# A hybrid decoder layer on one core: two-operand elementwise work moved to VectorE, and the loads of the merge moved

## The chip, the core and the metric

The kernel runs on one core of a Trainium2 chip. The metric is the device time of one execution in microseconds. A core has a matrix engine (TensorE, PE in the profile, its weight loads PEld), a vector engine (VectorE, DVE), a scalar engine (ScalarE, ACT), a general engine (GpSimd, POOL) and a sync engine (SyncE, SP), which here only issues DMA transfers. Each engine works off its own list of instructions in order and waits on semaphores for the others.

## The reference

One decoder layer is computed for a prompt of 2048 tokens and for 8 samples of 8 new tokens, 2112 tokens in all, with model width 1024. Cut to what matters:

```
h = rmsnorm(x, norm_attn);  p = h @ w_in          # 4608 columns: q, k, v, rwkv inputs, gates
o_attn = window attention with sinks(q, k, v)      # window 128, 8 heads, 2 kv heads
o_rwkv = rwkv7_mixer(p[rwkv part], state)          # recurrence, group norm, output gate
gates = sigmoid(p[gate part] + b_gate)
merged = gates[:1024] * (o_attn @ w_branch_attn) + gates[1024:] * (o_rwkv @ w_branch_rwkv)
x = x + merged @ w_out
u = rmsnorm(x, norm_ffn) @ w_ffn_in                # 2 x 2816 columns: gate half, value half
c = cb + causal conv of width 3 over the gate half
x = x + (gelu(c) * value half) @ w_ffn_out
y = rmsnorm(x, norm_final)                         # and the new caches and states
```

## The kernel before, in words

**Blocks and halves.** Everything is kept transposed, features on the 128 partitions and tokens along the free axis. The 2112 tokens are three blocks of 704, each in two halves of 384 and 320 tokens (HALF). A matmul of the large products is one 128x128 piece of weights against 384 or 320 columns.

**Split operands.** Float32 accuracy is had from a faster float format by splitting each operand into a rounded part (hi) and the rest (lo): `mm3` (L366) runs hi·hi, hi·lo and lo·hi for each of 8 pieces of weights, 24 matmuls for a bank (`psd`, three of them). `unit` brings 128x1024 weights: SP loads them to `wr` (L346), ScalarE makes hi with a cast (L347), and lo = raw − hi is a TENSOR_TENSOR (an instruction with two full operands) at L353. Every third unit's lo is one 128x1024 instruction on VectorE, the other two units' lo are two 128x512 instructions each on GpSimd. Activations are split by `split`, a cast at L357 and a subtraction at L358. There are two buffers for `wr` and two for the split weights `wp`, so a unit is split while the unit ahead of it is multiplied: 48 matmuls, 24 for each half.

**Stages.** `start` and `inputs(0..2)` compute the projections of the three blocks (matmuls named psd<-h). Then for each block come `branches` (the products with w_branch, psd<-o, and the gated sum: two `m` tiles from L1364, their addition at L1367, hi at L1369, lo at L1370), `merge` (the product with w_out, L1400, and the second norm) and `ffn_stage` (w_ffn_in, the conv and gelu, w_ffn_out at L1470), and last the final norm, whose scaling of the last block uses VectorE at L1538 and GpSimd at L1531.

**Background work.** Attention, the triangular inverses of the rwkv mixer (L1088, L1090, and two 128x1024 transposes on VectorE at L1094 and L1096 at the end of each of six), the recurrence over chunks and the group norm are Python generators in queues called streams. A recording layer (`tick`, `step`, `account`) weaves their instructions in between the matmuls of the stages when the program is written; it estimates each engine's time with the numbers in `cost` and takes a next step where these estimates leave room. `drain` runs a stream to its end, with nothing between its steps when no stage is being written. The order on every engine is thus fixed when the program is built.

**Around the merge of block 0.** The outputs of attention (`od`) and of the rwkv mixer (`rd`) go through DRAM. `gather` loads them as eight `ol` tiles (L1316, four buffers) and splits each into `os_` (L357, L358). For block 0 the stream "c" holds, during the third projections, `chunks(0)` and the first two query tiles of `attention(1)`; `gathered(0)` is pushed on it behind them, the last four gate products are written, and `drain("c")` ends it all. The rest of attention and the work of blocks 1 and 2 follow in the merge and the FFN. For blocks 1 and 2 the generator `ahead` gathers within the FFN of the block before. `load_x1` loads the residual x of the block with four DMAs when the third weight unit of `branches` is issued (L1376). The x after an FFN is stored to `xd` by a DMA that ScalarE issues (L1486), one for each half, and the final norm reads it back later.

## Time and profile before

| | |
|---|---|
| median of 3 runs | 3327.91 us (3327.47 to 3331.76) |
| profiled execution | 3327.79 us, its span 3326.0 us |
| mean granted clock of TensorE | 0.988 of full speed |
| PE busy | 3250.5 us (98%), 24072 matmuls |
| DVE busy | 1948.6 us (59%), 4058 instructions |
| ACT busy | 1213.4 us (36%) |
| POOL busy | 1010.1 us (30%) |

Read busy shares with the clock beside them: a matmul at the lower clock level counts as busy for twice as long. A row of a timeline holds neighbouring instructions of one line: start, elapsed time, engine, line, operation, tiles and shapes, count, and in brackets the idle time before it and who ended it. "ACTq" and "SPq" rows are the engines' issuing of DMAs; "DMA x<-y" as a releaser is the landing of a transfer.

### The profile page before, as it was taken

To read this page: it belongs to the slowest core of one execution; us is meant where nothing else is said; L and a number is where in the kernel's file an instruction comes from. 1 tells how busy PE (TensorE), PEld (TensorE's weight loads), DVE (VectorE), ACT (ScalarE), POOL (GpSimd) and SP (SyncE) were. 2 spreads that over 40 slices of the span, in tenths; PEclk is the share of its full clock that TensorE was granted. 3 is DMA by queue.
4 is the path that set the end of the run, shared out by engine and by line. 5 is a ranking of instruction groups with operands and counts; after the bars stand their busy time and mean duration, and the time that the engine had idled before them with its cause. 6 is when DMAs were issued, how large, how long until landed. Compare 5 with 4: busy or idle time off the path is not lost.

```text
span 3326.0 us, 60594 instructions
## 1 busy us (share of the span) xinstructions
PE 3250.5 (98%) x24072; PEld 3131.5 (94%) x24072; DVE 1948.6 (59%) x4058; ACT 1213.4 (36%) x2274; POOL 1010.1 (30%) x878
## 2 busy tenths in 40 slices
PE   8999998999999899999999999999999999999998
PEld 8998998999999789899999999999999999999998
DVE  7676568735563466577455558745456465444545
ACT  4455433333333567523232333332233233222223
POOL 3332433323223244132222254222122353222223
PEclk9999999999999899999999999999999999999999
DMA  4643443545653744233532363253313272122222
GB/s 136 182 141 117 140 152 118 146 130 159 200 171 119 221 144 118 73 80 105 153 118 87 111 225 96 82 168 110 112 65 130 70 257 70 64 70 70 70 65 75
DMA packets 335164, 408.96 MB, mean 123 GB/s; under 512 B 110496, under 2 KB 261152, under 8 KB 334624
## 3 DMA queue, kind: packets, MB, share of 16 engines
q1 hardware_dynamic: 330720, 399.31, 38.8%
q10 hardware_dynamic: 4160, 5.77, 0.5%
q8 instruction: 190, 3.11, 0.4%
q14 instruction: 94, 0.77, 0.1%
HBM read 307.55 MB, written 98.41 MB: 122 GB/s over the span
## 4 chain that ended last, share of the span: by engine, by line
PE 71%; DVE 3%; DMA 1%; issue 1%; ACT 0%; POOL 0%; SPq 0%; POOLq 0%; DVEq 0%; ACTq 0%
PE psd L366 62%; PE psr L694 1%; PE psr L743 1%; PE psc L1162 1%; PE psc L1195 1%; PE psc L1192 1%; DVE qt L1088 1%; DVE qb L1090 1%; PE psr L730 1%; DMA xd<-x 0%; PE psr L992 0%; PE psc L1019 0%; PE psc L1197 0%; PE psc L1291 0%; PE psc L1189 0%
## 5 line engine op out<-in xcount | busy, mean ns | idle before, releaser
L366 PE MATMUL psd<-o,wp 128*128 128x320 f32 (+1 forms) x8640 | 1453.6, 326 | 21.1 <-ACT o L357 10.8
L366 PEld LDWEIGHTS psd<-o,wp 128*128 128x128 f32 x8640 | 1400.9, 189 | 32.6 <-ACT o L357 11.8
L353 POOL TENSOR_TENSOR wp<-wr,wp 128x512 fp32r<-128x512 f32 x470 | 648.1, 1400 | 1675.7 <-ACT wp L347 1595.9
L366 PE MATMUL psd<-h,wp 128*128 128x320 f32 (+1 forms) x5184 | 918.1, 330 | 15.2 <-ACT wp L347 7.4
L366 PEld LDWEIGHTS psd<-h,wp 128*128 128x128 f32 x5184 | 838.4, 190 | 30.8 <-ACT wp L347 7.4
L347 ACT CAST wp<-wr 128x1024 fp32r<-128x1024 f32 x354 | 370.6, 1047 | 647.7 <-PE psd L366 587.6
L366 PE MATMUL psd<-ff,wp 128*128 128x384 f32 (+1 forms) x3168 | 526.7, 325 | 0.0
L366 PEld LDWEIGHTS psd<-ff,wp 128*128 128x128 f32 x3168 | 510.8, 188 | 3.1 <-DVE up L1434 0.2
L1470 DVE TENSOR_TENSOR x<-x,psd 128x384 f32<-128x384 f32 (+1 forms) x288 | 148.2, 519 | 236.9 <-PE psd L366 236.7
L1441 DVE TENSOR_TENSOR gb<-psd,rb 128x64 f32<-128x64 f32 (+2 forms) x154 | 70.5, 470 | 241.2 <-PE psd L366 223.7
L353 DVE TENSOR_TENSOR wp<-wr,wp 128x1024 fp32r<-128x1024 f32 x119 | 148.1, 1244 | 88.5 <-ACT wp L347 84.7
L1444 DVE SCALAR_TENSOR_TENSOR cc<-gb,pt,cc 128x704 f32<-128x704 f32 (+1 forms) x132 | 165.1, 1251 | 33.8 <-ACT cc L1442 33.0
L1442 ACT ACTIVATE cc<-gb,pt 128x64 f32<-128x64 f32 (+2 forms) x154 | 95.7, 636 | 188.6 <-DVE gb L1441 187.2
L407 POOL TENSOR_TENSOR acc<-acc,sq 128x320 f32<-128x320 f32 (+1 forms) x93 | 95.0, 1023 | 115.5 <-ACT sq L406 97.4
L1453 ACT ACTIVATE cc<-cc 128x704 f32<-128x704 f32 x66 | 52.4, 793 | 189.0 <-DVE cc L1444 119.1
L358 DVE TENSOR_TENSOR ff<-cc,ff 128x384 fp32r<-128x384 f32 (+1 forms) x132 | 92.9, 706 | 47.0 <-ACT ff L357 46.6
L1434 DVE TENSOR_TENSOR up<-psd,rb 128x384 f32<-128x384 f32 (+1 forms) x132 | 68.6, 520 | 51.7 <-PE psd L366 51.3
L357 ACT CAST ff<-cc 128x384 fp32r<-128x384 f32 (+1 forms) x132 | 63.9, 486 | 78.7 <-DVE cc L1456 78.1
L1090 DVE TENSOR_TENSOR qb<-qb,qt 128x31 f32<-128x31 f32 (+15 forms) x186 | 88.9, 478 | 4.1
L1088 DVE TENSOR_TENSOR qt<-nb,qb 128x31 f32<-128x31 f32 (+15 forms) x186 | 84.6, 455 | 3.2
L1367 POOL TENSOR_TENSOR m<-m 128x384 f32<-128x384 f32 (+1 forms) x48 | 48.8, 1018 | 118.4 <-DVE m L1364 85.2
L1456 DVE TENSOR_TENSOR cc<-cc,up 128x384 f32<-128x384 f32 (+1 forms) x132 | 71.2, 542 | 16.7 <-ACT cc L1453 13.5
(257 smaller groups left out, 3124.2 us busy)
## 6 DMA issues: line engine op xcount, KB each, us to landing
wr<-in_w_fi SPq DMA_DIRECT2D x132, 512.0 KB, 3.5
wr<-in_w_in SPq DMA_DIRECT2D x108, 512.0 KB, 4.0
wr<-in_w_fo SPq DMA_DIRECT2D x66, 512.0 KB, 3.5
cm<-md SPq DMA_DIRECT2D x33, 512.0 KB, 4.8
gt<-gd SPq DMA_DIRECT2D x48, 352.0 KB, 4.4
md<-m SPq DMA_DIRECT2D x48, 256.0 KB, 3.4
wr<-in_w_br SPq DMA_DIRECT2D x24, 512.0 KB, 4.7
wr<-in_w_out SPq DMA_DIRECT2D x24, 512.0 KB, 3.6
```

Of the source, the lines that this page charges most:

```text
L347: nc.scalar.copy(w[:, 0], raw)
L353: eng.tensor_tensor(w[:, 1, sl], raw[:, sl], w[:, 0, sl].bitcast(F32), op=ALU.subtract)
L358: (eng or self.nc.vector).tensor_tensor(lo, src, hi.bitcast(F32), op=ALU.subtract)
L366: nc.tensor.matmul(ps[:, :n], w[:, a, wk * 128:(wk + 1) * 128], act[:, k0 + k, b, c0:c0 + n], start=(start and k == 0 and j == 0), stop=(s ...
L407: eng.tensor_tensor(acc, acc, sq[:, :n], op=ALU.add)
L1088: nc.vector.tensor_tensor(tv, nb[:, s + 1:, s:s + 1].to_broadcast([P, k, s + 1]), qb[:, s:s + 1, :s + 1].to_broadcast([P, k, s + 1]), op=A ...
L1090: nc.vector.tensor_tensor(qb[:, s + 1:, :s + 1], qb[:, s + 1:, :s + 1], tv, op=ALU.add)
L1441: nc.vector.tensor_tensor(dst, view(ps, 0), view(rb, c0), op=ALU.mult)
L1442: nc.scalar.activation(view(c, c0), dst, ACT.Identity, bias=self.par("cb", f), scale=cw[2])
L1444: nc.vector.scalar_tensor_tensor(c[:, :npr], gb[:, u:u + npr], cw[u], c[:, :npr], op0=ALU.mult, op1=ALU.add)
L1456: nc.vector.tensor_tensor(cv, cv, up[:, c0:c0 + n], op=ALU.mult)
L1470: nc.vector.tensor_tensor(xv, xv, ps[:, :n], op=ALU.add)
```

## The change

1. All two-operand elementwise work that GpSimd did goes to VectorE: the lo of every weight unit (now one 128x1024 instruction), the splits of `parts`, `q2` and `h`, the additions of squares into `acc` for the norms, the products `kp` and `kb` of the mixer, and the addition of the two `m` tiles. Only the final norm's scaling of the last block stays on GpSimd. The estimates in `cost` and `account` drop their entries for such work on GpSimd.
2. For block 0 the eight `ol` loads are a generator of their own (`load_out`, now eight buffers), queued behind `chunks(0)` in the third projections in the place of the first part of attention(1); the splits (`gather`) are drained ahead of the last four gate products. Attention(1) runs whole in the merge.
3. `load_x1` loads one quarter of x at each of the units j = 2 to 5 of `branches` instead of all four at j = 2.
4. `gate_tiles` is a plain function that asks for its first two tiles when it is called, in the FFN, and no longer at the first `next`.
5. The copy of the window caches (`wks`, `wvs`) moves from the end of the third projections to the last FFN stage, and the `kt` tile of `mtile` comes from one pool for all blocks.

```diff
@@ unit, split, square
-        eng = nc.gpsimd if self.nw % 3 else nc.vector
-        self.nw += 1
-        step = 1024 if eng is nc.vector else 512
-        for u in range(0, 1024, step):
-            sl = slice(u, u + step)
-            eng.tensor_tensor(w[:, 1, sl], raw[:, sl], w[:, 0, sl].bitcast(F32), op=ALU.subtract)
+        nc.vector.tensor_tensor(w[:, 1], raw, w[:, 0].bitcast(F32), op=ALU.subtract)
...
-        (eng or self.nc.vector).tensor_tensor(lo, src, hi.bitcast(F32), op=ALU.subtract)
+        self.nc.vector.tensor_tensor(lo, src, hi.bitcast(F32), op=ALU.subtract)
...
-        eng.tensor_tensor(acc, acc, sq[:, :n], op=ALU.add)
+        self.nc.vector.tensor_tensor(acc, acc, sq[:, :n], op=ALU.add)
@@ account
-                start = max(t[engine], t["PE"])
-                if engine == "Pool" and type(ins).__name__ == "InstTensorTensor":
-                    self.locked = start, start + c
...
-                t[engine] = start + c
+                t[engine] = max(t[engine], t["PE"]) + c
@@ gather
+    def load_out(self, b, pool, bufs):
+
+        for k in range(8 + bufs - 1):
+            if k < 8:
+                t = pool.tile([P, T], F32, tag="ol", name="ol", bufs=bufs)
+                self.nc.sync.dma_start(t, self.od[b][:, k] if k < 4 else self.rd[b][k - 4])
+                self.ols.append(t)
+            if k >= bufs - 2:
+                yield
+
+    def gather(self, os_, loads):
+
         for k in range(8):
...
+            next(loads, None)
             yield 0.0 if k else 4.0
+            t = self.ols.popleft()
@@ branches
-            if j == 2:
-                self.load_x1(b, x)
+            if 2 <= j < 6:
+                self.load_x1(b, x, 2 * j - 4)
...
-                nc.gpsimd.tensor_tensor(m[0][:, :n], m[0][:, :n], m[1][:, :n], op=ALU.add)
+                nc.vector.tensor_tensor(m[0][:, :n], m[0][:, :n], m[1][:, :n], op=ALU.add)
@@ run
-            self.inputs(2, ep, [self.chunks(0), self.attention(1, 0, 256)], HOLD)
+            lp = []
+
+            def preload():
+                lp.append(self.pool("ol", side="right"))
+                yield from self.load_out(0, lp[0].__enter__(), 8)
+
+            self.inputs(2, ep, [self.chunks(0), preload()], HOLD)
...
-        self.push("c", self.gathered(0, os_))
+        self.drain("c")
+        self.push("c", self.gather(os_, iter(())))
...
-            self.push("c", self.attention(1, 256), self.attention(2), self.inverses(1), self.chunks(1))
+            self.push("c", self.attention(1), self.attention(2), self.inverses(1), self.chunks(1))
```

**TensorE where block 0's merge begins.** Before: the end of the gate products (psd<-h), the rest of the background (L992 of the mixer, L730 and L743 of attention), and the first products of `branches` (psd<-o).

```order
L366 MATMUL psd<-h,wp 128x320 x5
L992 MATMUL psr<-ar,kb 128x128
L730 MATMUL psr<-ct,s 128x128 x8
L743 MATMUL psr<-pT,v 64x256 x2
L730 MATMUL psr<-ct,s 128x128 x4
L743 MATMUL psr<-pT,v 64x256 x2
L730 MATMUL psr<-ct,s 128x128 x4
L743 MATMUL psr<-pT,v 64x256 x4
L366 MATMUL psd<-o,wp 128x384 x13
L366 MATMUL psd<-o,wp 128x320 x13
```

Now (L354 is `mm3`, L681 the scores of attention, L978 the mixer):

```order
L978 MATMUL psr<-ar,kb 128x128
L354 MATMUL psd<-h,wp 128x384 x13
L354 MATMUL psd<-h,wp 128x320 x24
...
L354 MATMUL psd<-h,wp 128x384 x24
L354 MATMUL psd<-h,wp 128x320 x24
L354 MATMUL psd<-o,wp 128x384 x24
L354 MATMUL psd<-o,wp 128x320 x24
L354 MATMUL psd<-o,wp 128x384 x24
L354 MATMUL psd<-o,wp 128x320 x8
L681 MATMUL psr<-k_12760,q_12759 128x256 x12
```

Before, 25 background matmuls stand alone between the last gate product and the first branch product; now gate and branch products stand next to each other, and attention(1) begins among the branch products.

**SyncE's queue at the same place.** Before (ol are the outputs to be gathered, k, v and q the tiles of attention, x the residual):

```order
L1316 DMA ol<-od_226 128x704 x4
L671 DMA v<-vd_224 128x128
L665 DMA q<-qd_218 64x4x128 x3
L1316 DMA ol<-rd_0_282 128x704
L1316 DMA ol<-rd_1_283 128x704
L665 DMA q<-qd_218 64x4x128
L1316 DMA ol<-rd_2_284 128x704
L671 DMA v<-vd_224 128x128
L1316 DMA ol<-rd_3_285 128x704
L671 DMA v<-vd_224 128x128
L1376 DMA x_12723<-in_xT 128x2x704 x4
L346 DMA wr<-in_w_br 128x1024
```

Now:

```order
L1281 DMA rd_3_284<-y 128x320
L1303 DMA ol<-od_225 128x704 x4
L1303 DMA ol<-rd_0_281 128x704
L1303 DMA ol<-rd_1_282 128x704
L1303 DMA ol<-rd_2_283 128x704
L1303 DMA ol<-rd_3_284 128x704
...
L339 DMA wr<-in_w_br 128x1024
L1367 DMA x_12416<-in_xT 128x2x704
L1296 DMA gd_15_275<-g 128x384
```

The eight loads now stand right behind the last store of the mixer's output, ahead of the loads of the branch weights, and x is asked for in single pieces among these.

**VectorE at the end of the fourth inverse, beside the FFN of block 0.** Before (L1094 and L1096 are the transposes, L1470 the addition of an FFN product to x, L353 the lo of a weight unit):

```order
L1470 TENSOR_TENSOR x_12723<-x_12723,psd 128x384
L1094 STREAM_TRANSPOSE t_17431<-qb 128x32x32
L1470 TENSOR_TENSOR x_12723<-x_12723,psd 128x320
L1096 STREAM_TRANSPOSE qinv<-qb 128x32x32
L353 TENSOR_TENSOR wp<-wr,wp 128x1024
```

Now (L1080 and L1082 the transposes, L1461 the addition, L341 the lo of a weight unit, L346 that of the FFN's activations):

```order
L341 TENSOR_TENSOR wp<-wr,wp 128x1024
L346 TENSOR_TENSOR ff<-cc,ff 128x320
L1461 TENSOR_TENSOR x_12416<-x_12416,psd 128x384 x2
L1461 TENSOR_TENSOR x_12416<-x_12416,psd 128x320
L1080 STREAM_TRANSPOSE t_17895<-qb 128x32x32
L1461 TENSOR_TENSOR x_12416<-x_12416,psd 128x320
L341 TENSOR_TENSOR wp<-wr,wp 128x1024
L1461 TENSOR_TENSOR x_12416<-x_12416,psd 128x384
L1082 STREAM_TRANSPOSE qinv<-qb 128x32x32
L1461 TENSOR_TENSOR x_12416<-x_12416,psd 128x320
```

Where one unit's lo stood behind the two transposes, one now stands ahead of them and one between.

## Rows read from the trace of the kernel before

**Rows 1.** The page's busy time of each engine over the whole span.

```profile
PE 3250.5 (98%) x24072; PEld 3131.5 (94%) x24072; DVE 1948.6 (59%) x4058; ACT 1213.4 (36%) x2274; POOL 1010.1 (30%) x878
```

**Rows 2.** The waits of TensorE: bank and line that waited, what it waited for, us in total, times, longest us.

```profile
PE psd L366 <- ACT o L357: 10.8, 2, 7.9
...
PE psr L1053 <- DVE rbk L1031: 5.8, 1, 5.8
PE psd L366 <- DVE m L1364: 5.6, 4, 3.7
```

**Rows 3.** The timeline of TensorE where block 0's merge begins.

```profile
1133.59 0.65 PE L730 MATMUL psr<-ct,s 128*128 128x128 f32 x4
...
1139.29 1.45 PE L743 MATMUL psr<-pT,v 128*64 128x256 f32 x8
1148.62 4.48 PE L366 MATMUL psd<-o,wp 128*128 128x384 f32 x12 [7.88 <-ACT o L357]
1156.05 8.06 PE L366 MATMUL psd<-o,wp 128*128 128x384 f32 x36 [2.95 <-ACT o L357]
1164.47 2.36 PE L366 MATMUL psd<-o,wp 128*128 128x384 f32 x12 [0.36 <-DVE m L1364]
1166.67 0.52 PE L694 MATMUL psr<-k,q 128*128 128x256 f32 x3
```

**Rows 4.** The timelines of SyncE's DMA issues (SPq) and of ScalarE at the same place.

```profile
1144.35 1.80 SPq L1316 DMA_DIRECT2D ol<-od  x4
...
1153.93 4.30 SPq L1376 DMA_DIRECT2D x<-in_xT  x4
...
1148.06 3.55 ACT L357 CAST o<-ol 128x384 fp32r<-128x384 f32 x8 [1.95 <-DMA ol<-od]
1155.49 0.87 ACT L357 CAST o<-ol 128x384 fp32r<-128x384 f32 x2 [3.88 <-DMA ol<-rd]
```

**Rows 5.** Windows: stretch, us, busy us (and instructions) of PE, PEld, DVE, ACT and POOL, granted clock, DMA share, GB/s.

```profile
1143.80:1161.00 17.20, 9.43 (x30) 8.56 (x31) 7.81 (x17) 8.58 (x18) 2.34 (x1) 0.50 0.95 293
...
1935.00:1952.00 17.00, 14.94 (x94) 14.68 (x92) 3.77 (x6) 3.86 (x8) 9.02 (x9) 1.00 1.03 387
...
2030.00:2070.00 40.00, 37.81 (x236) 37.37 (x234) 39.08 (x65) 13.28 (x23) 18.66 (x16) 1.00 0.18 53
...
564.55:570.30 5.75, 0.00 (x0) 0.00 (x1) 5.51 (x9) 1.72 (x3) 4.79 (x5) 0.71 0.23 76
```

**Rows 6.** The timeline of TensorE at the beginning of block 1's merge.

```profile
1934.31 15.63 PE L366 MATMUL psd<-o,wp 128*128 128x384 f32 x96
1953.67 8.91 PE L366 MATMUL psd<-o,wp 128*128 128x384 f32 x36 [3.73 <-DVE m L1364]
...
1963.34 23.40 PE L366 MATMUL psd<-o,wp 128*128 128x320 f32 x144
1987.77 1.29 PE L366 MATMUL psd<-o,wp 128*128 128x320 f32 x7 [1.03 <-DVE m L1364]
```

**Rows 7.** At the same place the timelines of ScalarE and SyncE, and, of the view of one tile, how long the stores xd<-x took.

```profile
1951.54 0.88 ACT L1369 ACTIVATE o<-m 128x384 fp32r<-128x384 f32 x2 [8.27 <-DMA xd<-x]
...
1934.83 2.23 SPq L1376 DMA_DIRECT2D x<-in_xT  x4
...
DMA to landing us min/median/max: 2.9/4.5/16.4
```

**Rows 8.** Groups of POOL's instructions by line: line, engine, operation, tiles, shapes, count, busy us, mean ns, idle us before them and who ended it.

```profile
L353 POOL TENSOR_TENSOR wp<-wr,wp 128x512 fp32r<-128x512 f32 x470 | 648.1, 1400 | 1675.7 <-ACT wp L347 1595.9 <-DVE S L1200 17.3 <-DVE o L358 15.3
L407 POOL TENSOR_TENSOR acc<-acc,sq 128x320 f32<-128x320 f32 (+1 forms) x93 | 95.0, 1023 | 115.5 <-ACT sq L406 97.4 <-DVE nwyr L387 5.0 <-ACT xs L837 4.3
...
L1367 POOL TENSOR_TENSOR m<-m 128x384 f32<-128x384 f32 (+1 forms) x48 | 48.8, 1018 | 118.4 <-DVE m L1364 85.2 <-DVE nwtd L391 7.9 <-DVE nm L631 5.6
```

**Rows 9.** Groups of VectorE's instructions: of the view by line, the lo of weights and the addition that reads a PSUM bank; of the views of single lines, the shortest, median and longest ns of L1444 (both operands in SBUF) and of L1470 (one of them in PSUM).

```profile
L353 DVE TENSOR_TENSOR wp<-wr,wp 128x1024 fp32r<-128x1024 f32 x119 | 148.1, 1244 | 88.5 <-ACT wp L347 84.7 <-POOL parts L358 1.5 <-issue 1.0
...
L1470 DVE TENSOR_TENSOR x<-x,psd 128x384 f32<-128x384 f32 (+1 forms) x288 | 148.2, 519 | 236.9 <-PE psd L366 236.7
...
L1444 DVE SCALAR_TENSOR_TENSOR cc<-gb,pt,cc x132: 872/952/1982, 1353.4 to 3288.4; 128x704 f32<-128x704 f32 x88, 128x640 f32<-128x640 f32 x44
...
L1470 DVE TENSOR_TENSOR x<-x,psd x288: 446/512/556, 1419.9 to 3308.8; 128x384 f32<-128x384 f32 x122, 128x320 f32<-128x320 f32 x22
```

**Rows 10.** The timelines of TensorE and VectorE at a unit whose lo came late.

```profile
2071.39 4.97 PE L366 MATMUL psd<-o,wp 128*128 128x384 f32 x18 [3.58 <-DVE wp L353]
...
2066.35 2.17 DVE L1094 STREAM_TRANSPOSE t<-qb 128x1024 f32<-128x1024 f32 x1
2068.41 1.87 DVE L1096 STREAM_TRANSPOSE qinv<-qb 128x1024 f32<-128x1024 f32 x1
2070.14 1.20 DVE L353 TENSOR_TENSOR wp<-wr,wp 128x1024 fp32r<-128x1024 f32 x1
```

**Rows 11.** The timelines of TensorE at the start and at the end of the kernel, and of POOL at its first two-operand instructions and at the end.

```profile
28.57 0.90 PE L1053 MATMUL psc<-ct,nwyd 128*128 128x128 f32 x3 [3.44 <-DVE nwyd L392]
...
3317.63 0.87 PE L1053 MATMUL psr<-ct,nwyd 128*128 128x128 f32 x3 [5.47 <-DVE nwyd L392]
...
15.30 2.79 POOL L353 TENSOR_TENSOR wp<-wr,wp 128x512 fp32r<-128x512 f32 x2 [14.42 <-ACT wp L347]
...
3319.05 3.31 POOL L1531 TENSOR_TENSOR x<-x,rbl 128x320 f32<-128x320 f32 x4 [3.35 <-ACT rbl L1527]
```

More of the change, by code (lines that the diff above doesn't have):

```diff
@@ L113, in __init__ @@
         self.pb = {k: pool("ps" + k, n, space=bass.MemoryType.PSUM) for k, n in (("d", 3), ("r", 3), ("c", 2))}
-        self.nw, self.ahead = 0, {}
+        self.ahead = {}
         self.streams = {}
@@ L232, in cost @@
             return 0.12 + 0.00084 * n
-        two = kind == "InstTensorTensor"
         if engine == "Pool":
-            return 0.1 + (0.0024 if two else 0.0009) * n
+            return 0.1 + 0.0009 * n
         if kind == "InstStreamTranspose":
@@ L270, in account @@
             else:
-                start = max(t[engine], t["PE"])
-                if engine == "Pool" and type(ins).__name__ == "InstTensorTensor":
-                    self.locked = start, start + c
-                elif engine == "DVE" and self.locked[0] <= start < self.locked[1] and not any(
-                        hasattr(a, "bass_ap") and a.bass_ap.tensor.name.startswith("ps") for a in ins.ins):
-                    start = self.locked[1] - 0.2
-                t[engine] = start + c
+                t[engine] = max(t[engine], t["PE"]) + c
                 self.chained = max(self.chained + c + 0.06, t[engine])
@@ L487, in start @@
         accs = []
[L488 removed]
+        for x, (c0, n) in zip(xs, HALF):
             acc = self.tp.tile([P, 384], F32, tag="acc", name="acc", bufs=2)
@@ L701, in head @@
             return s
-        items = [(t0, g) for t0 in range(t0, npr, 128) for g in range(2)]
-        fs = {t0: front(t0)}
+        items = [(t0, g) for t0 in range(0, npr, 128) for g in range(2)]
+        fs = {0: front(0)}
         yield 4.0
-        fs[t0] = halves(fs[t0])
-        if t0 + 128 < npr:
-            fr = front(t0 + 128)
+        fs[0] = halves(fs[0])
+        fr = front(128)
         yield 0.2
-        sm = {0: (yield from head(fs[t0], 0))}
+        sm = {0: (yield from head(fs[0], 0))}
         ready = {0: self.account()}
@@ L1310, in gate @@
         self.nc.sync.dma_start(self.gd[b][j][:, c0:c0 + n], t[:, :n])
-    def gather(self, b, os_, pool):
-        def load(k):
-            t = pool.tile([P, T], F32, tag="ol", name="ol", bufs=4)
-            self.nc.sync.dma_start(t, self.od[b][:, k] if k < 4 else self.rd[b][k - 4])
-            return t
-        ts = deque(load(k) for k in range(4 - 1))
+    def load_out(self, b, pool, bufs):
[7 more added lines that the diff above has]
+    def gather(self, os_, loads):
         for k in range(8):
-            if k + 4 - 1 < 8:
-                ts.append(load(k + 4 - 1))
-            t = ts.popleft()
+            next(loads, None)
             yield 0.0 if k else 4.0
+            t = self.ols.popleft()
             for c0, n in HALF:
@@ L1341, in load, with tiles @@
             gts.append(gt)
+        def tiles():
+            for j in range(8):
+                yield gts.popleft()
+                if j < 6:
+                    load(j + 2)
         for j in range(2):
             load(j)
-        for j in range(8):
-            yield gts.popleft()
-            if j < 6:
-                load(j + 2)
+        return tiles()
     def branches(self, b, os_, ms, gts, x):
@@ L1371, in branches, with load_x1 @@
         next(gts, None)
-    def load_x1(self, b, x):
+    def load_x1(self, b, x, k):
         with self.tc.issue_after(self.load):
-            for k in range(0, KT, 2):
-                self.nc.sync.dma_start(x[:, k:k + 2], self.i["xT"][:, k:k + 2, b * T:(b + 1) * T])
+            self.nc.sync.dma_start(x[:, k:k + 2], self.i["xT"][:, k:k + 2, b * T:(b + 1) * T])
     def merge(self, b, x, ms, xp, op):
@@ L1543, in done @@
             acc, xv = accs[hf][:, :n], x[:, j, c0:c0 + n]
-            self.square(acc, xv, j, n, nc.gpsimd if j < 6 else nc.vector)
+            self.square(acc, xv, j, n)
             if j == KT - 1:
@@ L1615, in inputs, with attention @@
                 nc.sync.dma_start(self.o["shs"], self.shs)
-                with self.tc.issue_after(self.load):
-                    for new, old in (("wks", "kcT"), ("wvs", "vcT")):
-                        nc.sync.dma_start(self.o[new][:, :, :120], self.i[old][:, :, 8:])
-    def attention(self, b, t0=0, t1=T):
+    def attention(self, b):
         with self.pool("att", side="right") as ap:
-            yield from self.attn_prompt(b, ap, t0, t1)
+            yield from self.attn_prompt(b, ap)
             if b == NB - 1:
@@ L1656, in ffn_stage @@
                 nc.sync.dma_start(self.cst_s, self.i["cvt"])
+                with self.tc.issue_after(self.load):
+                    for new, old in (("wks", "kcT"), ("wvs", "vcT")):
+                        nc.sync.dma_start(self.o[new][:, :, :120], self.i[old][:, :, 8:])
             self.ffn(b, x, h2, rb, fp, self.final_last(b, x, fp) if b == NB - 1 else self.final(b, x))
```

38 lines of the change are left out of this document (19 added, 19 removed).

## The prediction

> **What bounds the kernel now.** I read the page's busy times first: TensorE is busy for 3250.5 of 3326.0 us, so only 75.5 us of it are idle, and VectorE and GpSimd stand at 59% and 30% [rows 1]. The change leaves the matmuls as they are. It can therefore gain only TensorE's idle time and the time that matmuls lose at the lower clock; it can lose wherever TensorE begins to wait for VectorE. The list of TensorE's waits, read second, says where the large ones are: 10.8 us in two waits for the splits of the gathered outputs, 5.8 us for a chain of the mixer (rbk), 5.6 us in four waits for the gated sums m [rows 2]. The timelines of these places, read third, give the price with the clock in it. The pace at full clock is 96 matmuls in 15.63 us, 0.163 us each [rows 6].
>
> **The change, part by part.**
>
> *First merge (preload).* The branch products begin at 1148.62 after 7.88 us of idleness, and idle again for 2.95 and 0.36 us [rows 3]. Their 60 matmuls (12, 36, 12) take 4.48 + 8.06 + 2.36 = 14.9 us where the pace would give 60 x 0.163 = 9.8. The granted clock from 1143.8 to 1161.0 was 0.50 of full speed, the 1.2 GHz level, after the idle stretch [rows 5]. Idle 11.2 plus slow 5.1 makes 16.3 us. Who is late: the ol loads were issued only at 1144.35, between attention's loads, at a DMA share of 0.95, and the first cast of rd waited until 1155.49 for its load [rows 4, 5]. The new order issues all eight loads ahead of the last gate products, and gate products follow on TensorE, enough to cover 16 casts and 16 subtractions. I take all of it: **-16.3**. Bounds: -18, if the bare attention work ahead (1133.59 to 1140.74 [rows 3]) also loses its own waits; -3, if the last rd load still decides.
>
> *Second merge (x in four pieces, additions of m).* TensorE idles 3.73 us for m at 1953.67. The 36 matmuls after it take 8.91 us instead of 5.9, 3.0 too many, and 1.03 us more are lost at 1987.77 [rows 6]: 7.8 us. ScalarE's L1369, which makes the hi of m in a buffer that the old x held, waited 8.27 us for the store xd<-x; that store took 16.4 us where the median is 4.5; x's four loads were issued at 1934.83 beside it, and the DMA engines were full (share 1.03) [rows 5, 7]. With one quarter of x at a time the store should land in less than the 8 us that hide it (16.4 - 8.3). Later m chains shorten by half of an addition (1018 ns on POOL, about 519 on VectorE [rows 8, 9]). I take **-7.5**; bounds -7.8 and 0.
>
> *What VectorE takes over.* 235 units at 1.244 us = 292 us [rows 9]; 93 additions of squares and 48 of m at about 0.52 = 73 us [rows 8, 9]; the rest of POOL's 1010 us, 1010 - 648 - 95 - 49 = 218, part of it memsets that stay, at the ratio of the weight splits (1244 to 2 x 1400) at most 97 us. Together at most 462. What it gets back: L1444, both operands in SBUF, has 872 ns at its shortest and 1982 at its longest, while L1470, which reads a PSUM bank, stays between 446 and 556 [rows 9]. The long ones are what waiting out one POOL instruction of 1.0 to 1.4 us would add. Without any refund VectorE ends at 2411 us, 72%; I estimate 2050 to 2150, since POOL's two-operand instructions cover over a quarter of the span. The Trainium skill ("GPSIMD Engine Reference", section 1, Specifications) says that GpSimd's SBUF interfaces are shared with VectorE and that instructions of VectorE with two SBUF inputs contend for them; the rows agree, and by that rule the load would hardly rise, while without it it would rise by the 462. On average VectorE isn't the bound at either end. This bulk itself costs **0**: the cover is TensorE's own work. It is the order in VectorE's queue that can cost.
>
> *Weight units.* One unit feeds 48 matmuls, 144 / 3 in 23.40 / 3 = 7.8 us [rows 6]. After the cast, POOL needs 2 x 1.40 us for its lo, VectorE 1.24 [rows 8, 9], so two thirds of the units are ready 1.6 us sooner unless something stands ahead of them on VectorE. Behind a lo wait the next 24 matmuls of `mm3`, since they need lo. One late case is in the trace: two transposes (2.17 and 1.87 us) ahead of the lo at 2070.14, TensorE idle 3.58 us, then 18 matmuls in 4.97 us instead of 2.9: 5.6 us in all [rows 10]. There are six such pairs of transposes. One struck a unit when a third of the units were on VectorE; with all there, up to three would. The new order around the fourth pair has lo's ahead of and between the transposes, so the queue is shorter than it was at 2070. I take one more late unit, **+5.6**; bounds -5.6 (the old one goes) and +28 (five more).
>
> *The mixer's chain and smaller waits.* In the 5.75 us before rbk nine instructions of VectorE take 5.51 us, 0.61 each, while POOL is busy for 4.79 [rows 5]. Undisturbed they would be shorter, but POOL's work of that stretch now stands in the same queue. I take **-2.5** for this wait and **-2** for all smaller ones; bounds -20 and +5 together.
>
> *Start and end.* At 28.57 TensorE waits 3.44 us for a norm's chain on VectorE [rows 11]; additions of squares and two lo's (2 x 1.24) now enter that queue: **+1.5**, bounds -1 and +4. At the end the second half's chain (wait of 5.47 us) and its scaling on POOL (3.31 us for four) close the kernel [rows 11]. Now both halves' chains run side by side and both scalings come last, on POOL one after the other: some 2 us sooner for the chain and 3 us later for the second scaling, **+1**, bounds -2 and +3. Here a rule speaks against the change: by the Trainium skill ("GPSIMD Engine Reference", section 2.1, Instruction dispatch) the first use of a freshly loaded GpSimd kernel pays some 6 us of code loading. The first two-operand pair now falls at the end; at 15.30 it ran in 2.79 us, twice the mean of 1400 ns, after 14.42 us of idleness [rows 8, 11], so a charge at the call isn't seen, though one hidden in that idleness can't be excluded. It is a rival below.
>
> *Gate tiles, cache copies, the kt tile.* They move DMA issues only, at places where TensorE waits for nothing named here: 0, if their cover goes a wait like m's 3.7 us [rows 2].
>
> **Sum.** -16.3 - 7.5 - 2.5 - 2 + 5.6 + 1.5 + 1 = -20.2. The profiled execution took 3327.79 us, 1.8 more than its span and 0.1 below the median of the runs, so no correction is needed: 3327.8 - 20.2 = 3307.6, I say 3307.
>
> **The rivals.**
>
> *VectorE's chains speed up everywhere* (chance 0.2). TensorE's idle 75.5 us less the first merge (11.2), the second (4.8), the late unit (3.6) and some 12 at start and end leaves 44 us, for VectorE's chains in the main. If freeing VectorE halves them, 22 us go instead of the 4.5 counted: 3290. For it: 0.61 us per small instruction [rows 5]. Against it: 235 more weight splits stand in these queues.
>
> *Given back* (0.13). Four late units instead of one: 3307 + 3 x 5.6 = 3324, no change. For it: six pairs of transposes, and 39.08 of 40 us busy on VectorE before the late unit [rows 5]. Against it: the sooner lo everywhere else.
>
> *VectorE becomes the bound in dense stretches* (0.1, slower). The mechanism is a queue on VectorE ahead of a lo of more than 7.8 - 1.0 - 1.24, about 5.5 us. Each such unit costs 5.6 us. Without late units the sum is -25.8, so the fifth takes the gain and from the sixth on it is slower by over 0.2%; with seven it is 3327.8 - 25.8 + 39.2 = 3341.
>
> *The preload doesn't do what it says* (0.05): rd's last stores come so late that the gap remains, 3307 + 13 = 3320 to 3323.
>
> *A charge at POOL's first two-operand work* (0.03): a code load would delay the last scaling. From rows, it is at most the 14.42 us of idleness in which it could have hidden [rows 11]; by the page's 6 us the time would be 3313. Rows alone put it between 3307 and 3321.
>
> **Chances and range.** My forecast has 0.49, with its own range of 3296 to 3318. Changes within 0.2% (6.7 us) can't be told from no change here. Faster, below 3321.2: nearly all of the forecast, the first rival, and a part of the last two, 0.74. Within 0.2%: most of "given back" and edges, 0.14. Slower: the third rival and a little of the second, 0.12. The range of 3284 to 3331 takes in the first two rivals with a margin of 6 to 7 us each and leaves out the third.
>
> **What would show it.** Right: no idle before psd<-o at the first merge, full clock there, ol landed before the last gate products; stores xd of under 9 us and no 8 us wait at L1369's counterpart; L1444's counterpart with a longest near its shortest; one or two waits of psd for the lo of a weight unit, each after transposes. Wrong: five or more such waits (the third rival), psd waiting for ol (the fourth), a first scaling on POOL of far more than 0.9 us a piece at the end (the fifth), or the rbk wait longer than 5.8 us. The forecast is wrong as a whole if VectorE's busy time is above 2400 us, for then nothing was refunded.

## The result, and the profile after

The changed kernel takes 3282.97 us (3280.76 to 3284.38, 4 runs) where the kernel before took 3327.69 beside it: a ratio of 0.9864 (95% interval 0.9847 to 0.9881), 44.7 us less. The forecast was 3307 with a range from 3284 to 3331: the right sign, but under half the gain, and the time lies 1 us below the range. The profiled execution took 3283.15 us, its span 3281.2.

The page's busy times, which answer to [rows 1]:

```profile
PE 3242.3 (99%) x24072; PEld 3128.9 (95%) x24072; DVE 2029.4 (62%) x4596; ACT 1219.5 (37%) x2278; POOL 39.8 (1%) x104
```

TensorE's idle time, span less busy time, went from 3326.0 - 3250.5 = 75.5 us to 3281.2 - 3242.3 = 38.9: 36.6 of the 44.8 us by which the span shrank. The other 8.2 us are busy time, for the same 24072 matmuls: the granted clock rose from 0.988 to 0.992, so fewer of them ran at the lower level. VectorE, with 538 instructions more and all of the weight splits, is busy for only 81 us more.

What TensorE still waits for (bank and line, what it waited for, us in total, times, longest us), to be held against [rows 2]:

```profile
PE psd L354 <- ACT wp L340: 7.6, 1, 7.6
PE psc L1039 <- DVE nwyd L380: 4.7, 1, 4.7
PE psr L1039 <- DVE nwyd L380: 4.2, 2, 2.3
PE psd L354 <- DVE m L1356: 3.8, 1, 3.8
PE psd L354 <- DVE p L508: 2.5, 1, 2.5
PE psd L354 <- DVE xs L818: 1.7, 2, 0.9
PE psr L416 <- DVE acc L395: 1.6, 1, 1.6
PE psd L354 <- DVE gb L1432: 0.3, 1, 0.3
PE psd L354 <- DVE wp L341: 0.3, 1, 0.3
```

The splits of the gathered outputs, rbk, and the late lo of a weight unit have gone from the list; one wait for m of 3.8 us has stayed.

**First merge.** The timeline of TensorE, to be held against [rows 3]:

```profile
1079.73 23.31 PE L354 MATMUL psd<-h,wp 128*128 128x384 f32 x144
1102.88 13.26 PE L354 MATMUL psd<-o,wp 128*128 128x384 f32 x80
1115.98 1.59 PE L681 MATMUL psr<-k,q 128*128 128x256 f32 x12
```

Gate products (psd<-h) run into branch products (psd<-o) without idleness, and 80 of these take 13.26 us, 0.166 each: full clock.

**Second merge.** The timeline of TensorE, to be held against [rows 6]:

```profile
1897.26 15.55 PE L354 MATMUL psd<-o,wp 128*128 128x384 f32 x96
1916.58 23.58 PE L354 MATMUL psd<-o,wp 128*128 128x384 f32 x128 [3.77 <-DVE m L1356]
```

The timelines of ScalarE and SyncE there, to be held against [rows 7]:

```profile
1914.45 0.88 ACT L1361 ACTIVATE o<-m 128x384 fp32r<-128x384 f32 x2 [8.26 <-DMA xd<-x]
...
1896.23 0.39 SPq L1367 DMA_DIRECT2D x<-in_xT  x1
...
1900.20 0.48 SPq L1367 DMA_DIRECT2D x<-in_xT  x1
...
1907.86 0.48 SPq L1367 DMA_DIRECT2D x<-in_xT  x1
```

The view of the tile xd says how long its stores took:

```profile
DMA to landing us min/median/max: 3.1/4.2/16.4
```

After 96 matmuls TensorE idles as long as before (3.73, now 3.77 us). The first pieces of x stand apart in the code but were issued within 12 us, at 1896, 1900 and 1908, all beside the store, and the store took its 16.4 us again.

**VectorE.** The shortest, median and longest ns of three lines; the first answers to L1444 in [rows 9], the last to its L1470:

```profile
L1435 DVE SCALAR_TENSOR_TENSOR cc<-gb,pt,cc x132: 876/943/954, 1296.9 to 3242.9; 128x704 f32<-128x704 f32 x88, 128x640 f32<-128x640 f32 x44
...
L341 DVE TENSOR_TENSOR wp<-wr,wp x354: 1181/1224/1255, 7.6 to 3248.5; 128x1024 fp32r<-128x1024 f32 x177
...
L1461 DVE TENSOR_TENSOR x<-x,psd x288: 446/523/585, 1367.1 to 3262.9; 128x384 f32<-128x384 f32 x122, 128x320 f32<-128x320 f32 x22
```

The longest of the conv's first instruction fell from 1982 to 954 ns, and no weight split takes over 1255; the line that reads a PSUM bank is unchanged. Between the start of a cast and the end of its lo, worked out from the 354 pairs of these records, 99 in 100 take at most 4.1 us and the longest 6.3; before, 7.1 and 7.9 on VectorE, 7.0 and 8.3 on POOL.

**Start and end.** The timelines of TensorE and POOL, to be held against [rows 11]:

```profile
28.73 0.90 PE L1039 MATMUL psc<-ct,nwyd 128*128 128x128 f32 x3 [4.70 <-DVE nwyd L380]
...
3267.89 1.54 PE L1039 MATMUL psr<-ct,nwyd 128*128 128x128 f32 x6 [1.91 <-DVE nwyd L380]
...
3269.33 7.11 POOL L1522 TENSOR_TENSOR x<-x,rbl 128x320 f32<-128x320 f32 x8 [508.05 <-ACT rbl L1518]
```

The start waits 1.3 us longer. At the end the two norm chains run side by side with 1.91 us of waiting in the place of 5.47, and POOL's eight scalings come in one row, 0.89 us each, so that the end of the kernel is 11.8 us behind the last matmul (3267.89 + 1.54 to 3281.2).

### The profile page after: what moved, and what is told of

Same layout as the page of the kernel before. It is cut to its first block, busy times and chain, and to the rows that moved or that the text cites. A ratio compares the mean times of both kernels' runs of the same rounds, so it can differ in the third digit from the quotient of the medians.

```text
span 3281.2 us, 60116 instructions
## 1 busy us (share of the span) xinstructions
PE 3242.3 (99%) x24072; PEld 3128.9 (95%) x24072; DVE 2029.4 (62%) x4596; ACT 1219.5 (37%) x2278; POOL 39.8 (1%) x104
## 4 chain that ended last, share of the span: by engine, by line
PE 96%; DVE 1%; ACT 1%; DMA 1%; issue 0%; POOL 0%; SPq 0%; POOLq 0%; DVEq 0%; ACTq 0%
PE psd L354 83%; PE psr L978 2%; PE psr L681 1%; PE psr L729 1%; PE psr L716 1%; PE psc L1148 1%; PE psc L1178 1%; PE psc L1181 1%; PE psr L868 1%; DMA xd<-x 0%; PE psc L1005 0%; PE psr L966 0%; PE psc L1183 0%; PE psc L1175 0%; PE psr L1005 0%; PE psc L1277 0%
## 5 line engine op out<-in xcount | busy, mean ns | idle before, releaser
L354 PE MATMUL psd<-o,wp 128*128 128x320 f32 (+1 forms) x8640 | 1443.7, 325 | 4.1 <-DVE m L1356 3.8
L354 PEld LDWEIGHTS psd<-o,wp 128*128 128x128 f32 x8640 | 1392.6, 188 | 16.3 <-issue 8.0
L354 PE MATMUL psd<-h,wp 128*128 128x320 f32 (+1 forms) x5184 | 911.7, 329 | 12.3 <-ACT wp L340 7.6
L354 PEld LDWEIGHTS psd<-h,wp 128*128 128x128 f32 x5184 | 838.1, 189 | 25.4 <-ACT wp L340 7.6
L354 PE MATMUL psd<-ff,wp 128*128 128x384 f32 (+1 forms) x3168 | 536.1, 327 | 0.0
L341 DVE TENSOR_TENSOR wp<-wr,wp 128x1024 fp32r<-128x1024 f32 x354 | 432.8, 1222 | 164.9 <-ACT wp L340 157.8
L354 PEld LDWEIGHTS psd<-ff,wp 128*128 128x128 f32 x3168 | 515.3, 189 | 4.2 <-issue 1.0
L1461 DVE TENSOR_TENSOR x<-x,psd 128x384 f32<-128x384 f32 (+1 forms) x288 | 148.2, 519 | 200.7 <-PE psd L354 199.5
L1435 DVE SCALAR_TENSOR_TENSOR cc<-gb,pt,cc 128x704 f32<-128x704 f32 (+1 forms) x132 | 121.9, 924 | 2.2 <-ACT cc L1433 1.7
L1444 ACT ACTIVATE cc<-cc 128x704 f32<-128x704 f32 x66 | 52.4, 794 | 140.0 <-DVE cc L1435 82.9
L346 DVE TENSOR_TENSOR ff<-cc,ff 128x384 fp32r<-128x384 f32 (+1 forms) x132 | 68.5, 520 | 32.2 <-ACT ff L345 32.1
L1295 ACT ACTIVATE g<-psd,der 128x384 f32<-128x384 f32 (+1 forms) x64 | 35.5, 554 | 140.4 <-PE psd L354 89.2
L624 ACT ACTIVATE s<-s,nm 128x256 f32<-128x256 f32 (+2 forms) x136 | 65.8, 486 | 39.0 <-DVE nm L619 36.8
L1356 DVE SCALAR_TENSOR_TENSOR m<-gt,psd 128x384 f32<-128x384 f32 (+1 forms) x96 | 49.6, 518 | 36.3 <-PE psd L354 35.5
L823 ACT ACTIVATE xs<-psd,der 128x384 f32<-128x384 f32 (+1 forms) x56 | 31.1, 555 | 107.4 <-PE psd L354 107.4
L395 DVE TENSOR_TENSOR acc<-acc,sq 128x384 f32<-128x384 f32 (+1 forms) x126 | 65.2, 518 | 6.2 <-ACT sq L394 5.5
```

The source lines that it names most:

```text
L341: nc.vector.tensor_tensor(w[:, 1], raw, w[:, 0].bitcast(F32), op=ALU.subtract)
L346: self.nc.vector.tensor_tensor(lo, src, hi.bitcast(F32), op=ALU.subtract)
L354: nc.tensor.matmul(ps[:, :n], w[:, a, wk * 128:(wk + 1) * 128], act[:, k0 + k, b, c0:c0 + n], start=(start and k == 0 and j == 0), stop=(s ...
L624: nc.scalar.activation(s[:nq, h, :nk], s[:nq, h, :nk], ACT.Exp, bias=nm[:nq, h:h + 1], scale=0.125, accum_out=rs[:nq, h:h + 1])
L1435: nc.vector.scalar_tensor_tensor(c[:, :npr], gb[:, u:u + npr], cw[u], c[:, :npr], op0=ALU.mult, op1=ALU.add)
L1461: nc.vector.tensor_tensor(xv, xv, ps[:, :n], op=ALU.add)
```

## The experiments

All were timed beside the kernel before on the same chip; a time is compared with 3283 for the changed kernel by the ratios to before. Medians of one kernel differ by up to 3 us between chips.

### Which part brought the gain

**Part 1 alone**, on the kernel before: every hunk of the diff that turns `gpsimd` into `vector`, with the planner's numbers.

```diff
-        eng = nc.gpsimd if self.nw % 3 else nc.vector
...
+        nc.vector.tensor_tensor(w[:, 1], raw, w[:, 0].bitcast(F32), op=ALU.subtract)
```

> Part 1 alone on the kernel before. Theory A (POOL's two-operand instructions made VectorE's chains and queue slow, and that was most of the gain): the inner waits for VectorE and the late weight unit go, the gap at the first merge stays: about 3301 us (3295 to 3306), psd still waiting some 10 us for the splits of the gathered outputs. Theory B (the gain beyond the first merge's 16 us comes from moving attention and the loads): about 3320 us or more.

Measured: 3299.14 us, ratio 0.9915 (0.9900 to 0.9930), 28 us less than before. Its wait for the gathered outputs is even longer than in [rows 2]:

```profile
PE psd L354 <- ACT o L345: 16.0, 2, 9.1
```

So 28 us come without any preload. Theory A holds, theory B falls.

**Part 2 alone**, on the kernel before:

```diff
-            self.inputs(2, ep, [self.chunks(0), self.attention(1, 0, 256)], HOLD)
+            self.inputs(2, ep, [self.chunks(0), preload()], HOLD)
...
-        self.push("c", self.gathered(0, os_))
+        self.drain("c")
+        self.push("c", self.gather(os_, iter(())))
```

> Part 2 alone on the kernel before (preload, gather ahead of the last gate products, attention(1) whole in the merge). Theory A: only the first merge's 16 to 18 us go: about 3310 us (3306 to 3314), waits for VectorE's chains much as before, some 25 us. Theory B: 3295 us or less.

Measured: 3320.27 us, ratio 0.9980 (0.9970 to 0.9991): 6 us, a third of what both theories gave it at least. The wait for the gathered outputs is gone, but the timeline of TensorE has new waits 190 to 240 us behind the first branch product (1125.17), where attention(1) now runs whole in the merge:

```profile
1318.27 0.78 PE L1051 MATMUL psr<-ct,nwyd 128*128 128x128 f32 x3 [3.45 <-DVE nwtd L390]
...
1353.68 0.65 PE L741 MATMUL psr<-pT,v 128*64 128x256 f32 x4 [1.29 <-ACT pT L733]
...
1362.75 1.12 PE L741 MATMUL psr<-pT,v 128*64 128x256 f32 x4 [2.33 <-DVE pT L735]
```

These three are 7.1 us. In the changed kernel the same stretch has one wait of 2.3 us, the longest of `psr L1039` in the list above. Gathering early alone moves the wait; with a VectorE that isn't held up, most of it goes. That may be why the two parts together, below, bring 41 us by the medians and not 28 + 6; the intervals are too wide to show it.

**Parts 1 and 2 together**, without x in pieces, the gate tiles and the cache copy:

```diff
-            if 2 <= j < 6:
-                self.load_x1(b, x, 2 * j - 4)
+            if j == 2:
+                self.load_x1(b, x)
```

> Parts 1 and 2 together, without x in four pieces, the gate tiles' earlier request and the moved cache copy. If these three parts are worth nothing, 3283 us within 3, with the wait for m at the second merge still 3 to 4 us long; if x in pieces did help, 3288 us or more.

Measured: 3286.09 us (3283.44 to 3291.24), ratio 0.9883 (0.9866 to 0.9899), against 0.9864 (0.9847 to 0.9881). The intervals overlap: the difference of 3 us by the medians and 6 by the ratios isn't clear of noise, so the other three parts are worth nothing that this shows. The wait for m stands at 2.7 us here, a little under the 3 to 4 expected.

### Is it POOL that holds VectorE up, or the new order?

**POOL subtracts in vain.** Part 1 also gives every engine a new order, since the planner counts differently. This run keeps the changed kernel's order nearly as it is, and POOL does again what it did before for two units in three, into the spent raw tile, with nothing waiting for the result but the next load into that tile. The planner doesn't count it.

```diff
         nc.vector.tensor_tensor(w[:, 1], raw, w[:, 0].bitcast(F32), op=ALU.subtract)
+        if self.nw % 3:
+            for sl in (slice(0, 512), slice(512, 1024)):
+                nc.gpsimd.tensor_tensor(raw[:, sl], raw[:, sl], w[:, 0, sl].bitcast(F32), op=ALU.subtract)
+        self.nw += 1
```

> The changed kernel, but POOL again makes the lo of two units in three, in vain, from the same tiles into the spent raw buffer, and the planner's clock doesn't count it; the orders of TensorE, VectorE and ScalarE stay nearly those of the changed kernel. Theory A: the instructions of VectorE with two operands in SBUF get long again (L1435's counterpart up to 2000 ns, VectorE's busy time up by 200 us or more) and 10 to 25 us of waits return: 3293 to 3308 us. Theory C (not the waiting behind POOL but the new order of the instructions made the gain): 3283 us within 3.

Measured: 3319.71 us, ratio 0.9980 (0.9970 to 0.9989): 37 us slower than the changed kernel, well beyond what theory A expected. Its page's busy times:

```profile
PE 3258.2 (98%) x24072; PEld 3133.6 (94%) x24072; DVE 2241.8 (68%) x4596; ACT 1216.6 (37%) x2278; POOL 720.7 (22%) x576
```

The shortest, median and longest of the conv's first instruction there:

```profile
L1441 DVE SCALAR_TENSOR_TENSOR cc<-gb,pt,cc x132: 873/947/2035, 1316.0 to 3281.8; 128x704 f32<-128x704 f32 x88, 128x640 f32<-128x640 f32 x44
```

POOL's group of the vain subtractions, with its mean ns:

```profile
L346 POOL TENSOR_TENSOR wr<-wr,wp 128x512 f32<-128x512 f32 x470 | 679.9, 1467 | 2305.5 <-DVE wp L343 2183.6 <-DVE es L628 28.7 <-issue 17.8
```

The same 4596 instructions of VectorE take 212 us longer, the conv's longest is 2035 ns again, and nearly all of the gain is gone. The order is nearly that of the changed kernel: 4401 of VectorE's 4596 instructions follow each other as there. So theory C, the order, doesn't explain it. It isn't the kernel before again either, as VectorE here makes every lo and is held up besides. Of the 38.2 us that the span is longer, 22.3 are idle time of TensorE (3319.4 - 3258.2 against 38.9), as theory A expected; 15.9 are busy time for the same matmuls, at a mean granted clock of 0.988 in the place of 0.992, and that part its price left out.

Two rivals can be looked up in this trace. The spent tiles are free later, so weights could come late: but TensorE waits for a lo no longer than this:

```profile
PE psd L360 <- DVE wp L343: 1.1, 3, 0.5
```

And all of VectorE could be slower: but the addition that reads a PSUM bank keeps its times:

```profile
L1467 DVE TENSOR_TENSOR x<-x,psd x288: 447/525/595, 1386.8 to 3301.8; 128x384 f32<-128x384 f32 x122, 128x320 f32<-128x320 f32 x22
```

**POOL copies in vain**, first two copies of 512 columns, then two of 1024, with one operand each:

```diff
+            for q in range(2):
+                nc.gpsimd.tensor_copy(raw[:, 512:], raw[:, :512])     # d_one
+                nc.gpsimd.tensor_copy(raw, raw)                       # d_long
```

> The same with one-operand copies on POOL in the place of the subtractions (two of 512 columns for two units in three). Theory A, in the form that only two-operand work on POOL holds VectorE up: 3283 us within 3, L1435's counterpart at most 1000 ns. Rival (any work of POOL on SBUF holds VectorE up): a third to a half of what the two-operand copies of this run cost.

> As d_one, with two copies of 1024 columns for two units in three, each about twice as long as before (1.3 to 1.5 us), about as long as the subtractions of d_two. Theory F (an instruction of VectorE with two SBUF operands waits until POOL's running instruction ends, whatever that is): VectorE's busy time up by 150 us or more over the changed kernel, longest of the conv's first instruction 1.8 to 2.4 us, 3305 to 3325 us. Rival (only two-operand work on POOL does this to its full extent): below 3295 us and VectorE up by less than 110 us.

Measured: 3289.27 us, ratio 0.9879 (0.9864 to 0.9894), with the short copies; 3299.43 us, ratio 0.9928 (0.9908 to 0.9949), with the long ones. POOL's group of the short copies, and that page's busy times:

```profile
L346 POOL COPY wr<-wr 128x512 f32<-128x512 f32 x472 | 362.9, 769 | 2558.8 <-DVE wp L343 2445.5 <-DMA k<-kd 30.7 <-DVE nwtd L385 28.1
```

```profile
PE 3241.2 (99%) x24072; PEld 3125.0 (95%) x24072; DVE 2084.3 (63%) x4596; ACT 1220.1 (37%) x2278; POOL 401.0 (12%) x576
```

The same two of the long copies:

```profile
L346 POOL COPY wr<-wr 128x1024 f32<-128x1024 f32 x472 | 565.0, 1198 | 2416.4 <-DVE wp L343 2212.8 <-DMA k<-kd 36.7 <-DVE gb L1416 30.5
```

```profile
PE 3249.2 (99%) x24072; PEld 3128.7 (95%) x24072; DVE 2175.1 (66%) x4596; ACT 1218.3 (37%) x2278; POOL 602.1 (18%) x576
```

Copies hold VectorE up too: VectorE is 55 us busier with the short ones, and the conv's longest is 1374 ns where "two-operand work on POOL only" expected at most 1000; that form of theory A falls. The time of this run, 5 to 6 us above the changed kernel, isn't clear of noise, and is less than the third of 37 us that its rival expected.

A small instruction of the chain before rbk, with both operands in SBUF, shows it most plainly. Its shortest, median and longest ns in the kernel before, the changed kernel, and the runs with short copies, long copies and subtractions:

```profile
L390 DVE SCALAR_TENSOR_TENSOR nwtr<-nwyr x36: 158/170/1183, 53.7 to 999.4; 128x12 f32<-128x12 f32 x36
...
L378 DVE SCALAR_TENSOR_TENSOR nwtr<-nwyr x36: 154/170/184, 67.0 to 975.3; 128x12 f32<-128x12 f32 x36
...
L384 DVE SCALAR_TENSOR_TENSOR nwtr<-nwyr x36: 153/170/603, 69.6 to 978.1; 128x12 f32<-128x12 f32 x36
...
L384 DVE SCALAR_TENSOR_TENSOR nwtr<-nwyr x36: 157/170/1043, 69.4 to 983.5; 128x12 f32<-128x12 f32 x36
...
L384 DVE SCALAR_TENSOR_TENSOR nwtr<-nwyr x36: 158/170/1295, 73.9 to 990.9; 128x12 f32<-128x12 f32 x36
```

The longest of a 170 ns instruction comes near one whole instruction of POOL, whose shortest take 608, 1036 and 1264 ns in the last three runs.

VectorE's added time over the changed kernel is 55, 146 and 212 us for 472 instructions of 0.769 us, 472 of 1.198 and 470 of 1.467. If whoever meets a running instruction waits for its rest, the added time goes with the count times the length squared, halved: 140, 339 and 506. The quotients are 0.39, 0.43 and 0.42, nearly one number, where POOL's busy time (363, 565, 680 us) would give 0.15, 0.26 and 0.31. POOL's mean lengths hold waits of its own; with its medians (0.626, 1.054 and 1.344 us) the quotients are 0.59, 0.56 and 0.50, still closer together than with busy time. So the length of POOL's instruction decides, by three runs, and whether it has one operand or two doesn't show. The Trainium skill ("SBUF — State Buffer", section SBUF: two separate sides) has this as a rule: an instruction of VectorE with two SBUF inputs and one of GpSimd that reads SBUF lock the shared ports against each other, and the first to come keeps them for its whole length. The three quotients agree with it. The time of the kernel was expected at 3305 to 3325 for the long copies and came to 3299, between the two theories' ranges; VectorE's 146 us are just under the bound of 150, and the conv's longest is 1802 ns, at the low end of 1.8 to 2.4 us. More instructions stand in another order in that run (4126 of VectorE's 4596 follow each other as in the changed kernel), so its time is less sure than its busy time.

### How much the weight units are of it

**The weight units alone** on VectorE, and **all but the weight units**, each on the kernel before:

```diff
-            eng.tensor_tensor(w[:, 1, sl], raw[:, sl], w[:, 0, sl].bitcast(F32), op=ALU.subtract)
+        nc.vector.tensor_tensor(w[:, 1], raw, w[:, 0].bitcast(F32), op=ALU.subtract)      # u_only
...
-                nc.gpsimd.tensor_tensor(m[0][:, :n], m[0][:, :n], m[1][:, :n], op=ALU.add)
+                nc.vector.tensor_tensor(m[0][:, :n], m[0][:, :n], m[1][:, :n], op=ALU.add) # r_only, and the other small ones
```

> The kernel before with only the lo of the weight units moved to VectorE, the other two-operand work left on POOL and in the planner's account. Theory A (VectorE is held up in proportion to POOL's busy time): the units are 648 of about 1000 us of it, so about two thirds of the 28 us of part 1: 3308 us (3302 to 3313). Theory E (what mattered were the small instructions of POOL in the mixer's and norms' own chains): 3320 us or more.

> The other side: everything of part 1 but the weight units, which stay on POOL two in three. Theory A: a third of the 28 us, 3317 us (3312 to 3322). Theory E: most of them, 3305 us or less.

Measured: 3292.79 us, ratio 0.9901 (0.9887 to 0.9916), with the units alone; 3315.53, ratio 0.9966 (0.9953 to 0.9979), with the rest alone. The second fits theory A, the first is a miss: the units alone bring 34 us where 19 were expected, by the medians even more than all of part 1, though these two intervals overlap. Neither is a clean measure: the gap at the first merge differs between these kernels:

```profile
PE psd L361 <- ACT o L352: 8.4, 2, 7.8
```

That is the wait of the run with the units alone; part 1 has 16.0 us there, the run with the rest alone 4.1, and the kernel before 10.8. So the fit of the second may be luck in part, and how the 28 us divide isn't settled by these runs. Where this gap is gone for both, the comparison is cleaner: **the units alone with the preload and late pieces of x**, against the same with all of part 1 (x_late, below).

> Only the weight units on VectorE, the rest of the two-operand work left on POOL, with the preload and the late pieces of x. Theory A (POOL's work costs VectorE time wherever it is): slower than x_late, 3280 to 3290 us. Rival (once the units are off POOL the rest may stay, as the run with the units alone was 6 us faster than the whole of part 1): 3268 to 3275 us.

Measured: 3283.84 us, ratio 0.9872 (0.9857 to 0.9887), against 0.9845 for x_late: 9 us slower, as theory A has it. That POOL's smaller work holds TensorE's chains up is not shown by it, though: the planner gives this kernel another order, part 5 is missing in it, and TensorE idles hardly longer (3281.9 - 3245.7 = 36.2 us against 3270.7 - 3235.3 = 35.4 in x_late). The difference stands in its busy time.

### The second merge

**Pieces of x two units later**, on the changed kernel, and alone on the kernel before:

```diff
-            if 2 <= j < 6:
-                self.load_x1(b, x, 2 * j - 4)
+            if j >= 4:
+                self.load_x1(b, x, 2 * j - 8)
```

> The changed kernel with the four pieces of x asked for at units 4 to 7 in the place of 2 to 5. Theory D (at the second merge the store of the old x is slow because the new x is loaded beside it, in pieces or not): the second store xd lands in 13 us or less instead of 16.4, the wait for m falls below 1 us, 3276 to 3280 us. Rival (the store is slow by itself or by the other loads): store still over 15 us, 3283 us within 2.

> The kernel before with x in four pieces at the units 4 to 7 and nothing else. If the second merge's term of the prediction (7.5 us) was right in size and place and only the cure in the change came too early, this takes it: the second store xd in 11 us or less, the wait of 3.7 us for m gone, 3318 to 3322 us. Rival (in x_late the gain came only together with the freed VectorE, which makes m sooner): 3324 us or more.

Measured: 3274.95 us, ratio 0.9845 (0.9830 to 0.9860), and 3319.97, ratio 0.9985 (0.9975 to 0.9995). The timeline of TensorE in the first of the two, and in the view of the tile xd how long its stores took:

```profile
1893.32 31.87 PE L354 MATMUL psd<-o,wp 128*128 128x384 f32 x197
```

```profile
DMA to landing us min/median/max: 3.1/4.5/10.5
```

The same in the second:

```profile
1934.04 21.84 PE L366 MATMUL psd<-o,wp 128*128 128x384 f32 x134
```

```profile
DMA to landing us min/median/max: 2.9/4.6/10.3
```

The store lands in 10.5 us, and 197 branch products run without a wait. From 1915.4 to 1922 the granted clock is 1.00, where the changed kernel, behind its wait, has 0.50. The order of TensorE and ScalarE is the same in both, so what x_late gains, 8 us by the medians and 6 by the ratios, belongs to the loads. The two intervals overlap at their ends, but the slowest of its runs (3278.42) is under the fastest of the changed kernel (3280.76). Theory D holds; the time is 1 us better than its range. On the kernel before the gain is 5 us, as expected.

**One scaling of each half at the end moved from POOL to VectorE**, on x_late:

```diff
-            for k in range(1, KT, 2):
+            for k in range(1, KT - 2, 2):
...
-            for k in range(0, KT, 2):
+            for k in (7, 0, 2, 4, 6):
```

> x_late with one scaling of each half at the end moved from POOL to VectorE (10 instructions on VectorE, 6 on POOL in the place of 8 and 8). If POOL's scaling closes the kernel: 1.5 us less than x_late, some 3273 us; if the stores do: the same as x_late.

Measured: 3274.86 us, ratio 0.9847 (0.9833 to 0.9862), the same as x_late, though 1.5 us is less than these times can tell. POOL's work at the end:

```profile
3262.03 5.36 POOL L1522 TENSOR_TENSOR x<-x,rbl 128x320 f32<-128x320 f32 x6 [508.07 <-ACT rbl L1518]
```

It ends at 3267.4, 6.8 us before the end of that run's span (3274.2); in x_late POOL ends 4.7 us before it (3266.0 of 3270.7). POOL is done sooner and the end doesn't follow, which points to the stores as what closes the kernel.

## Why the prediction missed the size

**First merge, -16.3: right.** No idleness, full clock, the gathered outputs landed in time. It stood on a condition that the prediction didn't name: attention(1) then runs whole in the merge, and on the kernel before most of the gain was lost again (part 2 alone, 6 us).

**Second merge, -7.5: right in place and price, wrong in the cure.** The step that failed is "with one quarter of x at a time the store should land in less than the 8 us that hide it". The pieces are tied to the issue of the weight loads, and the loads of units 2 to 4 are issued within 12 us, while the store runs. It is read from SyncE's timeline and not from the loop over j. The wait of 3.73 us stayed (3.77), and the term brought nothing in the place of 7.5. Two units later the wait went, for 5 us on the kernel before and 6 to 8 on the changed one.

**VectorE's load: right in kind, beyond the estimate.** The prediction gave 2050 to 2150 us, at most 2411; it came to 2029.4. The Trainium skill ("GPSIMD Engine Reference", section 1, Specifications) names the shared interfaces and the instructions of VectorE with two SBUF inputs. The trace agrees: the conv's instruction falls from 1982 to 954 ns at its longest, and the line that reads PSUM stays.

**Weight units, +5.6: wrong in sign.** The failed step is "with all there, up to three would" be late. It took one late case, with a third of the units on VectorE, as the measure for all. None came: 99 in 100 are ready in 4.1 us, the longest in 6.3, and TensorE waits 0.3 us for a lo in all. The late unit at 2071 went with its 5.6 us: a term mis-sized by 11. What ended that unit's wait isn't shown. The transposes are as long as before (up to 2.3 us), and with VectorE held up again by the vain subtractions 99 in 100 take 5.5 us and still no lo is over 0.5 us late; so the order around the transposes, which the prediction named, is the likelier cause.

**The mixer's chain and smaller waits, -4.5: the largest miss.** The failed step is its price: the prediction halved one wait and took 2 us for the rest. What the other terms leave of the 44.7 us is 44.7 - 16.3 - 5.6 + 0.9 = 23.7 (first merge, late unit, start and end), five times as much and beyond the bound of -20. It is a remainder, with the slow clock behind each wait in it. Nearly all of these waits went: rbk isn't in the list, and inside the kernel only m, one norm's 2.3 us and 2.3 us of xs, gb and wp are left of the waits for VectorE. Part 1 alone brought 28 us, with a longer gap at the first merge than before, so the size fits. The first rival, chains that speed up everywhere, was the one that came. Its 3290 kept the +5.6 for a late unit and the 7.5 of the second merge; without the late units and without that gain it is 3290 - 11.2 + 7.5 = 3286. The prediction had the evidence: nine small instructions of 0.61 us each before rbk [rows 5], and a longest of twice the shortest at L1444 [rows 9]. It put what was held up into VectorE's busy time and asked whether that was the bound. The price lay in the latency of chains of dependent instructions: in the chain before rbk one of 170 ns took up to 1183 ns, and in the changed kernel it takes at most 184.

**Start +1.5 and end +1: about right.** The norm's wait at the start rose by 1.3 us. At the end waits of 2.75 and 5.47 became 1.61 and 1.91, and the time behind the last matmul grew by 4.3 us (from 7.5, 3326.0 less 3318.5, to 11.8): together 0.4 us less.

**The charge on POOL's first two-operand work: not seen.** The first scaling began at 3269.33 after 508 us without work, and eight took 7.11 us, 0.89 each, near the 0.83 at the end before (3.31 us for four). The Trainium skill ("GPSIMD Engine Reference", section 2.1, Instruction dispatch) gives some 6 us for the first call of freshly loaded code; the trace shows none here.

**The slower rival** needed six late units or more, and "given back" four. There was none over 0.3 us.

## What to carry to other kernels

Before asking whether an engine has room, look at the shortest and longest of its instructions: where lines with two SBUF operands vary by a factor of two and lines that read PSUM don't, as here, another engine may be holding it up, and every dependent chain pays. Work that looks free on an idle GpSimd then costs latency on VectorE, and the more, the longer each instruction is; a test with work in vain, in nearly the same order, tells this from the effects of a new order. When a transfer is late because others run beside it, read from the queue's timeline when these are really issued before counting on a later line of code, and when early work frees a place, look what moves into it.

## What the runs showed of the hardware that was not expected

The prediction had taken it that two-operand work on POOL holds VectorE up; copies with one operand do it too. VectorE's added time went about with the square of the length of POOL's instructions (55, 146 and 212 us for 472, 472 and 470 instructions of 0.769, 1.198 and 1.467 us), as if VectorE waited for the rest of the one that runs; a 170 ns instruction took up to 603, 1043 and 1295 ns. And 354 weight splits on VectorE were ready sooner than 119 had been there: the longest from cast to lo fell from 7.9 to 6.3 us.
